# Bias terms in bf16, scatters on four banks and a new order ahead of the expert loop of a decoder layer

## The chip, the core and the metric

The kernel runs on one core of a Trainium2 chip. The metric is device time in microseconds (us) of one execution, as the median of several. The engines are TensorE (PE, whose weight loads are shown apart as PEld), VectorE (DVE), ScalarE (ACT), GpSimd (POOL) and SyncE (SP), which here only issues DMAs. Each takes its instructions in order; they meet at semaphores. ACT can issue DMAs too, on a queue of its own.

## What is computed

One decoder layer for 256 tokens of width 1024: attention with a relative-position bias, an output projection, a layer norm, then a mixture of 32 experts of which each token takes four, and a second layer norm. All inputs and weights are float32.

```
h = layer_norm(ALPHA * x + attention(x, w_in, w_out, rel_bias))
logits = h @ w_router + b_router
top_logit, top_e = top_k(logits, 4);  gate = softmax(top_logit)
for each expert e, for the rows xb of the tokens that chose it:
    g, u = split(xb @ w_gu[e] + b_gu[e])          # 1024 -> 2 x 1024
    g = min(g, 7);  u = clip(u, -7, 7)
    y = (g * sigmoid(1.702 * g) * (u + 1)) @ w_down[e] + b_down[e]
out = layer_norm(ALPHA * h + sum over the four experts of gate * y)
```

The weights of one expert are 8 MB (w_gu) and 4 MB (w_down), and all 32 experts are read, 403 MB in all.

## The kernel before

**Weights.** A pool of 13 slots of 2 MB holds the weights. Three of the slots are taken for the whole attention part (`xhl`, `BT_xT`, `QT_KTt`), the last two of them to the end, so 11 are left for the experts. `prefetch` issues one DMA on SP's queue for each slot that is given back by `done` or `drop`, in the order in which the pieces are used: for each expert four pieces of w_gu (`gu`) and two of w_down (`dn`), so 192 pieces of 2 MB. SP waits at each issue until the slot's last reader is through.

**Attention.** The projections run in two terms (a high part that ACT casts at line 176, a low part that DVE subtracts at line 165, in `split`), one half block ahead of PE. `rel_bias` writes the bias row to DRAM and reads it back spread over the partitions, both on SP's queue, ahead of further loads. The output projection runs in four chunks of `w_out` (`out_part(j, ...)`, j = 0 to 3); chunk j + 1 is split while chunk j is multiplied. Behind chunk 0 the expert biases are loaded: `b_gu` (32 x 2048) and `b_dn`, each once, into rows of the freed half `QT` (`biases`). 

**Router.** While the last chunk is multiplied, tokens come in two tiles t of 128 rows. `residual`, `count` and `Stats` make the norm; `rows_T` transposes the rows on PE and ACT copies them; `logits`, `top_experts` and `positions` give each token its place in its experts' blocks of 64. `stats[0].normal` runs on POOL for tile 0 and on ACT for tile 1. `first_gather(t)` then multiplies the rows by one-hot columns into banks tp0 and tp1 (opened by a matmul of zeros), so that the first pair's tokens lie transposed in `xg`. `filler(n)` issues n matmuls of zeros.

**Expert loop.** Experts go in pairs p, s = 0, 1. For expert e = 2p + s PE does: the bias (`stage1_bias`: four float32 matmuls of a one-hot over the 32 rows of `b_gu` into banks hg and hu), stage 1 (`stage1`, line 651: 64 columns of tokens against 512 columns of weights, two halves of the array side by side), then, while DVE and ACT make the SwiGLU, the scatter of the previous pair (`pair_scatter`, only s = 0: four matmuls into banks o0, o1, o0, o1, each added to `acc` by DVE at line 702) or the gather of the next pair (`pair_gather`, only s = 1: two quarters), then four transposes of the activation (`act_T`, line 668), a copy by ACT (line 669), and stage 2 (`stage2`, line 679). For s = 1 `pair_slots_T` transposes the pair's gates too. At e = 17 and 19 `add_residual` adds ALPHA * h and the down biases, at e = 21 `overflow_list` counts tokens beyond 64. Behind the loop, `more_blocks` would run such blocks, and the second norm ends the kernel.

**Order.** The schedule is manual: each engine runs its instructions in the order of the Python code.

Of the kernel before, what the change touches and what calls it, by code (L numbers as in the profile page):

```python
# [60 lines left out]
def tile_decoder_layer(ctx: ExitStack, tc, a, out):  # L61
# [152 lines left out]

    hctx = ExitStack()
# [14 lines left out]
    zeros = hp.tile([128, 512], BF, name="zeros")  # L230
# [27 lines left out]
    def rel_bias():  # L258
        pr = bank("tp2")
        nc.tensor.matmul(pr[:H, :256], rb, oh, start=True, stop=True)  # L260
        nc.vector.tensor_copy(rrow[:, 127:383], pr[:H, :256])
        nc.sync.dma_start(rd, rrow)
        nc.sync.dma_start(BT, bass.AP(tensor=rd.tensor, offset=rd.offset,
                                      ap=[[1, 128], [383, H], [1, S]]))
        nc.sync.dma_start(c, a["consts"])
        nc.sync.dma_start(router.rearrange("p k e -> p (k e)"), a["router"])

# [80 lines left out]
    def softmax(hh):  # L348
        ps = P[hh]
        p = hp.tile([128, 384], F32, name="p", bufs=3)  # L350
# [37 lines left out]
    for n in range(12):  # L388
# [69 lines left out]

    def router_weights():

        p = hp.tile([128, 384], F32, name="p", bufs=3)
        wb, cols = p[:, :256].rearrange("p (k e) -> p k e", k=KT), p[:, 256:320].rearrange("p (i e) -> p i e", i=2)
# [8 lines left out]
    for j in range(3):  # L471
        split_next(("out", 0, j))
        if j == 2:
            reserve[0] = 0
        for t in range(2):
            out_part(j, t, range(2 + t))
        done_split(("out", 0, j))
        if j == 1:
            router_weights()
        if j == 0:  # L480
            bgu, bdn, gT = biases[:NE], biases[NE:2 * NE, :D], biases[NE:2 * NE, D:D + S]
            nc.sync.dma_start(bgu, a["b_gu"])
            nc.sync.dma_start(bdn, a["b_dn"])
            bgu = bgu.rearrange("p (q c) -> p q c", q=4)
# [35 lines left out]
    def open_gather():  # L520

        for ps in first_ps:
            nc.tensor.matmul(ps, zeros[:, :128], zeros, start=True, stop=False)

    def filler(n):

        ps = bank("o0")
        for i in range(n):
            nc.tensor.matmul(ps, zeros[:, :128], zeros, start=i == 0, stop=i == n - 1)
# [19 lines left out]
    def stage1_bias(onehot_e):  # L549
        hgu = [bank(n) for n in ("hg", "hu")]  # L550
        for i in range(2):
            for s in range(2):
                nc.tensor.matmul(hgu[i][s * 64:(s + 1) * 64], onehot_e, bgu[:, 2 * i + s, :],  # L553
# [45 lines left out]
    pp = positions(0)  # L599
    hgu = stage1_bias(ident[:NE, 0:1].to_broadcast([NE, CAP]))  # L600
    top_experts(1)
    read_positions(0, pp)
    stats[1].normal_act(x[:, 1])
    pair_onehots(0, OH, slice(0, 1))
    first_ps = [bank("tp0"), bank("tp1")]
    open_gather()
    pp = positions(1)
    first_gather(0)
    read_positions(1, pp)
    pair_onehots(0, OH, slice(1, 2))  # L610
    filler(2)
# [17 lines left out]
    def pair_gather(OH):  # L629
        xg = mp.tile([128, KT, 2 * CAP], F32, name="xg")  # L630

        def quarter(q):
            ps = tp_tile()
# [31 lines left out]
    def act_T(act):  # L665
        ps = tp_tile()
# [18 lines left out]
    def pair_slots_T(Gd, GT=None):  # L685
        ps = tp_tile()
# [5 lines left out]
        if GT is None:  # L692
            GT = mp.tile([128, 2, 2, 2 * CAP], F32, name="GT")
# [9 lines left out]

    def pair_scatter(GT, Y, t, fresh):
        for cb in range(2):
            po = o_tile()
# [9 lines left out]
    def add_residual(i):  # L716

        cs = HALVES[i]
        if i == 0:
            ps = tp_tile()  # L720
            for t in range(2):
                nc.tensor.matmul(ps[NE:2 * NE, t * 128:(t + 1) * 128], gates[:, t], ident, start=True, stop=True)
            nc.scalar.copy(gT, ps[NE:2 * NE, :256])
# [36 lines left out]
    def more_blocks():  # L760
# [9 lines left out]
        with tc.For_i(0, n_reg, 1):  # L770
# [21 lines left out]
            sel_e = mp.tile([NE, 1], F32, name="sel_e")  # L792
            nc.vector.tensor_scalar(sel_e, c[:NE, C_PM:C_PM + 1], ec[:NE, 0:1], None, op0=OP.is_equal)
# [24 lines left out]
            hgu = stage1(lambda k: xg[:, k, :CAP], gu_chunk, stage1_bias(sel_e.to_broadcast([NE, CAP])),  # L818
# [16 lines left out]
    for p in range(NE // 2):  # L835
        ahead_pair = p + 1 < NE // 2
        for s in range(2):
            e = 2 * p + s
            look_ahead = ahead_pair and s == (p > 0)
            if e:  # L840
                hgu = stage1_bias(ident[:NE, e:e + 1].to_broadcast([NE, CAP]))
# [6 lines left out]
            if GT is not None and not s:  # L848
                for t in range(2):
                    pair_scatter(GT, Y, t, p == 1)  # L850
            if e in (17, 19):
                add_residual(e == 19)
            if e == 21:
                overflow_list()
            if look_ahead:
                xg_next, quarter = pair_gather(OH)
                quarter(0)
                if not s:
                    quarter(1)
            act_T(act)  # L860
            if s:
                GT = pair_slots_T(Gd)
                if ahead_pair:
                    if look_ahead:
                        quarter(1)
                    xg = xg_next
                    Gd = pair_gates(e + 1, OH)
# [101 lines left out]
```

## Time and profile before

| | us |
|---|---|
| median of 3 runs (lowest to highest) | 1072.66 (1072.33 to 1074.49) |
| the profiled execution, its own time | 1072.28 |
| its span, first to last instruction | 1070.5 |
| PE busy | 1016.2 (95%) |
| DVE, ACT, POOL busy | 264.1, 176.8, 7.4 |
| moved by DMA | 425.21 MB, 397 GB/s in the mean |

Steps are made against the span of 1070.5 us; 1.8 us lie around it. A busy share says what an engine did, not whether the end waited for it: PE is busy 95% of the span, and the DMA engines move 425 to 429 GB/s in nearly every slice of the expert loop. Which of the two sets the end is read from who waits for whom, and from when a weight lands against when it is used.

### The profile page before, as it was taken

Reading aid. Unit: us, or ns where it says so; the run is one execution under the profiler, and the core shown is the slowest. Engines: PE = TensorE matmul, PEld = TensorE weight load, DVE = VectorE, ACT = ScalarE, POOL = GpSimd, SP = SyncE. Lnnn points to the kernel's source line nnn. Section 1 sums busy time; section 2 is a strip of 40 time slices with the busy share of each in tenths; the row PEclk is TensorE's granted clock in tenths of the full one; section 3 lists DMA queues with packets and bytes.
Section 4 is the critical chain, followed back from the end, with each engine's and each line's share of the span. In section 5 each row is a group of like instructions: output and inputs, shape, how many; then the busy total and the mean of one; then the engine's idle time right before and its main releaser. Section 6 shows DMA issues by size and latency. Waiting matters only on the chain. (4 is left out here: it accounts for less than half of the span.)

```text
span 1070.5 us, 11658 instructions
## 1 busy us (share of the span) xinstructions
PE 1016.2 (95%) x5008; PEld 452.2 (42%) x5008; DVE 264.1 (25%) x554; ACT 176.8 (17%) x343; POOL 7.4 (1%) x8
## 2 busy tenths in 40 slices
PE   9999999999999999999999999999999999999994
PEld 8988743343434333343434343343434343434331
DVE  5576511212121211112121232212221212121204
ACT  5455311010101011010101010010101010101012
POOL 0000100000000000000000000000000000000001
PEclk9999899999999999999999999999999999999998
DMA  8995799999999999999999999999999999999931
GB/s 298 419 425 197 305 415 428 426 426 427 425 426 428 426 427 427 425 429 426 426 428 427 425 428 429 425 427 428 424 428 426 426 427 427 426 427 427 426 135 40
DMA packets 33108, 425.21 MB, mean 397 GB/s; under 512 B 3640, under 2 KB 5088, under 8 KB 7424
## 3 DMA queue, kind: packets, MB, share of 16 engines
q1 hardware_dynamic: 32784, 423.41, 93.9%
q10 hardware_dynamic: 272, 1.05, 0.3%
q8 instruction: 40, 0.66, 0.2%
q14 instruction: 12, 0.10, 0.0%
HBM read 423.38 MB, written 1.06 MB: 396 GB/s over the span
## 5 line engine op out<-in xcount | busy, mean ns | idle before, releaser
L651 PE MATMUL hg<-w,xg 128*64 128x512 f32 x960 | 248.2, 595 | 0.0
L651 PE MATMUL hu<-w,xg 128*64 128x512 f32 x960 | 246.6, 592 | 0.0
L679 PE MATMUL yp<-w,QT_KTt 128*64 128x512 f32 x1008 | 228.3, 599 | 10.6 <-ACT QT_KTt L669 10.6
L658 DVE TENSOR_SCALAR QT_KTt<-hg 128x512 f32<-128x512 f32 x32 | 22.1, 692 | 665.8 <-PE hg L651 665.8
L679 PEld LDWEIGHTS yp<-w,QT_KTt 128*64 128x64 f32 x1008 | 70.9, 138 | 145.5 <-issue 129.1
L651 PEld LDWEIGHTS hg<-w,xg 128*64 128x64 f32 x960 | 66.2, 137 | 144.4 <-issue 143.6
L651 PEld LDWEIGHTS hu<-w,xg 128*64 128x64 f32 x960 | 68.8, 137 | 137.2 <-issue 137.2
L659 ACT ACTIVATE QT_KTt<-QT_KTt 128x512 f32<-128x512 f32 x32 | 20.1, 629 | 459.8 <-DVE QT_KTt L658 459.8
L683 ACT COPY QT_KTt<-yp 64x512 f32<-64x512 f32 x63 | 36.5, 579 | 244.4 <-PE yp L679 237.4
L707 PE MATMUL o<-QT_KTt,GT 128*128 128x512 f32 x120 | 59.5, 618 | 12.8 <-DVE BT_xT L702 12.0
L637 PE MATMUL tp<-OH,BT_xT 128*128 128x128 f32 x480 | 62.5, 285 | 5.7 <-ACT xg L547 5.7
L637 PEld LDWEIGHTS tp<-OH,BT_xT 128*128 128x128 f32 x480 | 56.9, 195 | 20.3 <-issue 10.4
L165 DVE TENSOR_TENSOR whl<-w,whl 128x1024 fp32r<-128x1024 f32 (+1 forms) x36 | 38.3, 1103 | 22.6 <-ACT whl L176 22.6
L702 DVE TENSOR_TENSOR BT_xT<-o,BT_xT 128x512 f32<-128x512 f32 x60 | 40.0, 687 | 11.4 <-PE o L707 11.0
L707 PEld LDWEIGHTS o<-QT_KTt,GT 128*128 128x128 f32 x120 | 20.3, 188 | 51.8 <-DVE BT_xT L702 27.8
L176 ACT CAST whl<-w 128x1024 fp32r<-128x1024 f32 (+1 forms) x36 | 32.7, 955 | 14.3 <-PE tp L437 5.5
L553 PE MATMUL hg<-QT_KTt,c 32*64 32x512 f32 x128 | 35.0, 623 | 0.0
L545 DVE TENSOR_SCALAR xg<-tp,c 128x128 f32<-128x128 f32 x60 | 20.5, 405 | 53.7 <-PE tp L637 53.7
L553 PE MATMUL hu<-QT_KTt,c 32*64 32x512 f32 x128 | 33.6, 602 | 0.0
L669 ACT COPY QT_KTt<-tp 128x512 f32<-128x512 f32 x32 | 18.9, 590 | 73.6 <-PE tp L668 73.6
L547 ACT ACTIVATE xg<-tp,c 128x128 f32<-128x128 f32 x60 | 22.5, 456 | 34.0 <-PE tp L637 34.0
L668 PE MATMUL tp<-c,QT_KTt 128*128 128x128 f32 x128 | 20.3, 282 | 5.9 <-DVE QT_KTt L662 4.3
(250 smaller groups left out, 716.9 us busy)
## 6 DMA issues: line engine op xcount, KB each, us to landing
w<-in_w_gu SPq DMA_DIRECT2D x128, 2048.0 KB, 23.6
w<-in_w_dn SPq DMA_DIRECT2D x63, 2048.0 KB, 21.6
w<-in_w_in SPq DMA_DIRECT2D x3, 2048.0 KB, 15.8
w<-in_w_in SPq DMA_DIRECT2D x4, 1024.0 KB, 11.1
w<-in_w_out SPq DMA_DIRECT2D x2, 2048.0 KB, 24.8
w<-in_w_dn SPq DMA_DIRECT2D x4, 512.0 KB, 25.3
w<-in_w_in SPq DMA_DIRECT2D x4, 256.0 KB, 5.6
w<-in_w_in SPq DMA_DIRECT2D x2, 512.0 KB, 8.6
```

Source lines behind the costliest of these rows:

```text
L165: nc.vector.tensor_tensor(lo[:, s], w[:, s], hi[:, s].bitcast(F32), op=OP.subtract)
L176: nc.scalar.copy(o, i)
L545: nc.vector.tensor_scalar(o, i, g, b, op0=OP.mult, op1=OP.add)
L547: nc.scalar.activation(o, i, AF.Identity, scale=g, bias=b)
L553: nc.tensor.matmul(hgu[i][s * 64:(s + 1) * 64], onehot_e, bgu[:, 2 * i + s, :], start=True, stop=False)
L637: nc.tensor.matmul(ps[:, k * 128:(k + 1) * 128], h[:, t, kk * 128:(kk + 1) * 128], OH[:, t].rearrange("p s c -> p (s c)"), start=t == 0, s ...
L651: nc.tensor.matmul(hgu[i][s * 64:(s + 1) * 64], xg(k), w[:, kk, q * 512:(q + 1) * 512], start=False, stop=k == KT - 1)
L658: nc.vector.tensor_scalar(g7, hgu[0], LIMIT, None, op0=OP.min)
L679: nc.tensor.matmul(y_ps[s], aT[:, kk % 4, kk // 4, :], w[:, k, HALVES[s ^ swap]], start=kk == 0, stop=kk == KT - 1)
L683: copy(Y[s * 64:(s + 1) * 64, s ^ swap, :], y_ps[s])
L702: nc.vector.tensor_tensor(d, po, d, op=OP.add)
L707: nc.tensor.matmul(po, GT[:, cb, t, :], Y[:, cb, :], start=True, stop=True)
```

## The change

**Biases.** `b_gu` is loaded three times, into 96 rows. `bias_terms` makes three bf16 terms of it whose sum is the float32 value: ACT casts (96 x 2048), POOL subtracts (64 x 2048), ACT casts again (64 x 2048), POOL subtracts again (32 x 2048). The bias matmul then is one bf16 matmul over 96 rows, with a bf16 one-hot `sel`, in place of a float32 one over 32 rows. `bgu` lies in the memory of the softmax's three `p` tiles (pool `pp`, tag p3).

**Down bias.** `b_dn` is loaded later, at expert 15, into a weight slot `late` that is held until expert 19; `reserve` keeps that slot free from expert 14 on.

**Scatters and transposes.** The four scatters of a pair go to banks o0, o1, tp0, tp1, the fourth behind `act_T`. The gather's quarters have banks tp0 and tp1 for themselves, `act_T` tp2, `pair_slots_T` o0, and this comes ahead of `act_T`. The second quarter comes behind `act_T`. `xg` and `GT` move into `biases`.

**Attention and router.** The two DMAs of the relative bias go from SP's queue to ACT's, one and two half blocks later. The zeros shrink to 128 columns, read four times over. Fillers: two ahead of `positions(0)`, three behind `open_gather`, three instead of two ahead of `first_gather(1)`.

```
-        nc.sync.dma_start(rd, rrow)
-        nc.sync.dma_start(BT, bass.AP(tensor=rd.tensor, offset=rd.offset, ...))
+    def rel_bias_out():
+        nc.scalar.dma_start(rd, rrow)
+    def rel_bias_in():
+        nc.scalar.dma_start(BT, bass.AP(tensor=rd.tensor, offset=rd.offset, ...))
...
+        if n == 2:
+            rel_bias_out()
+        if n == 3:
+            rel_bias_in()
...
+    bgu = pp.tile([3 * NE, 2 * D], BF, name="bgu", tag="p3")
+    sel = small("sel", NE, 3 * NE, BF)
+    def bias_terms(i):
+        if i == 0:
+            nc.scalar.copy(bgu, biases[:3 * NE])
+            nc.gpsimd.tensor_tensor(biases[:2 * NE], biases[:2 * NE], bgu[:2 * NE], op=OP.subtract)
+            nc.vector.tensor_scalar(sel, e32[:3 * NE], c[:3 * NE, C_PM:C_PM + 1], None, op0=OP.is_equal)
+        else:
+            nc.scalar.copy(bgu[:2 * NE], biases[:2 * NE])
+            nc.gpsimd.tensor_tensor(bgu[NE:2 * NE], biases[NE:2 * NE], bgu[NE:2 * NE], op=OP.subtract)
...
         done_split(("out", 0, j))
+        if j == 0:
+            for i in range(3):
+                nc.sync.dma_start(biases[i * NE:(i + 1) * NE], a["b_gu"])
         if j == 1:
             router_weights()
-        if j == 0:
-            bgu, bdn, gT = biases[:NE], biases[NE:2 * NE, :D], biases[NE:2 * NE, D:D + S]
-            nc.sync.dma_start(bgu, a["b_gu"])
-            nc.sync.dma_start(bdn, a["b_dn"])
+            bias_terms(0)
+        if j == 2:
+            bias_terms(1)
...
+    first_ps = [bank("tp0"), bank("tp1")]
+    filler(2)
+    pp0 = positions(0)
+    hgu = stage1_bias(sel[:, 0:1].to_broadcast([3 * NE, CAP]))
...
     open_gather()
+    filler(3)
...
-    filler(2)
+    filler(3)
     first_gather(1)
...
-    def pair_scatter(GT, Y, t, fresh):
-        for cb in range(2):
-            po = o_tile()
+    def pair_scatter(GT, Y, t, fresh, cbs=range(2)):
+        for cb in cbs:
+            po = bank((("o0", "o1"), ("tp0", "tp1"))[t][cb])
...
-            if GT is not None and not s:
-                for t in range(2):
-                    pair_scatter(GT, Y, t, p == 1)
+            scatter = GT is not None and not s
+            if scatter:
+                pair_scatter(GT, Y, 0, p == 1)
+                pair_scatter(GT, Y, 1, p == 1, (0,))
+            reserve[0] = int(e == 14)
+            if e == 15:
+                late = slot("late")
+                nc.sync.dma_start(late[:NE, :D], a["b_dn"])
...
-            act_T(act)
             if s:
                 GT = pair_slots_T(Gd)
+            act_T(act)
+            if scatter:
+                pair_scatter(GT, Y, 1, p == 1, (1,))
+            if look_ahead:
+                quarter(1)
```

On ACT, from the cast of out-projection chunk 1 to the first copies of the transposed rows (`hg`, `hu`), there stood before (`whl` holds the split weights):

```order
L176 CAST whl<-w 128x1024 x2
L423 ACT_TABLE_LOAD
L176 CAST whl<-w 128x1024 x4
L176 COPY QT_KTt<-hg 128x4x128
L176 COPY QT_KTt<-hu 128x4x128
```

And now stands on ACT at the same place:

```order
L176 CAST whl<-w 128x1024 x2
L433 ACT_TABLE_LOAD
L176 CAST whl<-w 128x1024 x2
L475 CAST bgu<-QT_KTt 96x2048
L176 CAST whl<-w 128x1024 x2
L479 CAST bgu<-QT_KTt 64x2048
L176 COPY QT_KTt<-hg 128x4x128
L176 COPY QT_KTt<-hu 128x4x128
```

The first cast of the biases has moved in ahead of the casts of chunk 3, and the second ahead of the copies of the transposed rows. On POOL the two subtractions stand ahead of the normalisation of tile 0 (line 207).

On PE, from the end of stage 1 of expert 2 to the bias of expert 3, there stood before (`o` and `tp` are banks, `yp` stage 2's):

```order
L651 MATMUL hu<-w,xg 64x512 x2
L707 MATMUL o_1522<-QT_KTt,GT 128x512
L707 MATMUL o_1525<-QT_KTt,GT 128x512
L707 MATMUL o_1528<-QT_KTt,GT 128x512
L707 MATMUL o_1531<-QT_KTt,GT 128x512
L668 MATMUL tp_1534<-c,QT_KTt 128x128 x4
L679 MATMUL yp<-w,QT_KTt 64x512 x16
L553 MATMUL hg<-QT_KTt,c 64x512 x2
```

And now stands on PE at that place:

```order
L677 MATMUL hu<-w,QT_KTt 64x512 x2
L733 MATMUL o_1531<-QT_KTt 128x512
L733 MATMUL o_1534<-QT_KTt 128x512
L733 MATMUL tp_1537<-QT_KTt 128x512
L694 MATMUL tp_1540<-c,QT_KTt 128x128 x4
L733 MATMUL tp_1546<-QT_KTt 128x512
L705 MATMUL yp<-w,QT_KTt 64x512 x16
L577 LDWEIGHTS sel
L577 MATMUL hg<-bgu,sel 64x512
```

The fourth scatter has moved behind the transposes, the last two have other banks, and the bias reads `bgu`.

## Rows read from the trace of the kernel before

**Rows 1.** Page, section 2: GB/s moved by the DMA engines, 40 equal slices.
```profile
GB/s 298 419 425 197 305 415 428 426 426 427 425 426 428 426 427 427 425 429 426 426 428 427 425 428 429 425 427 428 424 428 426 426 427 427 426 427 427 426 135 40
```

**Rows 2.** Waits of PE: engine, line, waited for: total us, times, longest us.
```profile
PE o L707 <- DVE BT_xT L702: 12.0, 14, 1.2
```

**Rows 3.** Windows: stretch us, length, busy us by engine (instructions), PE clock, DMA share, GB/s.
```profile
101.00:102.00 1.00, 0.94 (x7) 0.72 (x6) 0.41 (x3) 0.59 (x1) 0.00 (x0) 1.00 1.02 213
118.00:127.00 9.00, 8.66 (x36) 5.32 (x36) 3.13 (x19) 1.52 (x2) 0.70 (x1) 0.62 0.97 407
173.00:178.00 5.00, 4.76 (x20) 1.97 (x22) 0.90 (x4) 1.07 (x2) 0.00 (x0) 0.66 1.02 433
972.00:999.00 27.00, 26.50 (x140) 11.33 (x138) 4.85 (x12) 4.25 (x9) 0.00 (x0) 1.00 1.01 427
```

**Rows 4.** Timeline of SP's queue, three issues: start us, us, engine, line, operation, tile.
```profile
94.46 0.38 SPq L482 DMA_DIRECT2D QT_KTt<-in_b_gu  x1
132.80 0.33 SPq L138 DMA_DIRECT2D w<-in_w_dn  x1
991.73 0.33 SPq L138 DMA_DIRECT2D w<-in_w_gu  x1
```

**Rows 5.** DMA view of those issues, same order: KB, last number us to landing.
```profile
QT_KTt<-in_b_gu SPq DMA_DIRECT2D x1, 256.0 KB, 9.3
w<-in_w_dn SPq DMA_DIRECT2D x1, 2048.0 KB, 8.9
w<-in_w_gu SPq DMA_DIRECT2D x1, 2048.0 KB, 27.6
```

**Rows 6.** Timeline of PE: experts 2 and 3, last expert: start us, us, line, form.
```profile
182.73 1.07 PE L553 MATMUL hg<-QT_KTt,c 32*64 32x512 f32 x4
184.59 1.08 PE L651 MATMUL hg<-w,xg 128*64 128x512 f32 x4
198.48 1.98 PE L707 MATMUL o<-QT_KTt,GT 128*128 128x512 f32 x4
201.27 1.98 PE L707 MATMUL o<-QT_KTt,GT 128*128 128x512 f32 x4 [0.81 <-DVE BT_xT L700]
204.36 1.08 PE L679 MATMUL yp<-w,QT_KTt 128*64 128x512 f32 x4 [0.67 <-ACT QT_KTt L669]
227.13 2.05 PE L637 MATMUL tp<-OH,BT_xT 128*128 128x128 f32 x16
232.75 0.65 PE L679 MATMUL yp<-w,QT_KTt 128*64 128x512 f32 x2
239.77 1.07 PE L553 MATMUL hg<-QT_KTt,c 32*64 32x512 f32 x4
1039.11 1.03 PE L651 MATMUL hg<-w,xg 128*64 128x512 f32 x4
```

**Rows 7.** Timeline ahead of the expert loop: ACT, PE and POOL.
```profile
101.41 2.00 ACT L176 CAST whl<-w 128x1024 fp32r<-128x1024 f32 x2 [3.56 <-PE tp L437]
107.30 0.40 PE L434 MATMUL o<-whl,xhl 128*128 128x512 f32 x1
112.05 0.58 ACT L176 COPY QT_KTt<-hg 128x512 f32<-128x512 f32 x1 [8.64 <-PE hg L454]
114.57 4.13 POOL L207 TENSOR_SCALAR BT_xT<-BT_xT,rs_a 128x512 f32<-128x512 f32 x2 [114.12 <-DVE rs_a L203]
126.80 0.59 PE L529 MATMUL o<-zeros 128*128 128x512 bf16 x2
127.23 1.95 PE L535 MATMUL tp<-BT_xT 128*128 128x128 f32 x16
129.11 1.08 PE L651 MATMUL hg<-w,BT_xT 128*64 128x512 f32 x4
```

**Rows 8.** Line 898 by source: POOL multiplication, min/median/max ns.
```profile
L898 POOL TENSOR_TENSOR BT_xT<-BT_xT,gb_sq x2: 1402/1550/1698, 1060.3 to 1062.3; 128x512 f32<-128x512 f32 x2
```

**Rows 9.** Page, section 5, one group: busy us, mean ns, idle before.
```profile
L165 DVE TENSOR_TENSOR whl<-w,whl 128x1024 fp32r<-128x1024 f32 (+1 forms) x36 | 38.3, 1103 | 22.6 <-ACT whl L176 22.6
```

More of the change, by code (lines that the diff above doesn't have):

```diff
@@ L229, in tile_decoder_layer @@
     rrow = hp.tile([H, 383], F32, name="rrow")
-    zeros = hp.tile([128, 512], BF, name="zeros")
+    zeros = hp.tile([128, 128], BF, name="zeros")
+    zeros4 = zeros[:, None, :].to_broadcast([128, 4, 128])
+    p3 = pp.tile([128, 3, 384], F32, name="p3", tag="p3")
     router = hp.tile([128, KT + 1, NE], F32, name="router")
@@ L349, in softmax @@
         ps = P[hh]
-        p = hp.tile([128, 384], F32, name="p", bufs=3)
+        p = p3[:, hh % 3]
         st = hp.tile([128, 8], F32, name="sst", bufs=3)
@@ L457, in tile_decoder_layer @@
     sums = small("sums", 2 * NE)
+    bgu = pp.tile([3 * NE, 2 * D], BF, name="bgu", tag="p3")
[8 more added lines that the diff above has]
+            nc.gpsimd.tensor_tensor(bgu[NE:2 * NE], biases[NE:2 * NE], bgu[NE:2 * NE], op=OP.subtract)
     def router_weights():
-        p = hp.tile([128, 384], F32, name="p", bufs=3)
-        wb, cols = p[:, :256].rearrange("p (k e) -> p k e", k=KT), p[:, 256:320].rearrange("p (i e) -> p i e", i=2)
+        wb, cols = first[:, 1536:1792].rearrange("p (k e) -> p k e", k=KT), first[:, 1792:1856]
+        cols = cols.rearrange("p (i e) -> p i e", i=2)
         ps = bank("yp")
@@ L522, in open_gather @@
         for ps in first_ps:
-            nc.tensor.matmul(ps, zeros[:, :128], zeros, start=True, stop=False)
+            nc.tensor.matmul(ps, zeros, zeros4, start=True, stop=False)
     def filler(n):
@@ L528, in filler @@
         for i in range(n):
-            nc.tensor.matmul(ps, zeros[:, :128], zeros, start=i == 0, stop=i == n - 1)
+            nc.tensor.matmul(ps, zeros, zeros4, start=i == 0, stop=i == n - 1)
     def first_gather(t):
@@ L629, in pair_gather @@
     def pair_gather(OH):
-        xg = mp.tile([128, KT, 2 * CAP], F32, name="xg")
+        xg = biases[:, :1024].rearrange("p (k c) -> p k c", k=KT)
         def quarter(q):
-            ps = tp_tile()
+            ps = bank(("tp0", "tp1")[q])
             for k in range(4):
@@ L665, in act_T @@
     def act_T(act):
-        ps = tp_tile()
+        ps = bank("tp2")
         for j in range(4):
@@ L685, in pair_slots_T @@
     def pair_slots_T(Gd, GT=None):
-        ps = tp_tile()
+        ps = bank("o0")
         for cb in range(2):
@@ L692, in pair_slots_T @@
         if GT is None:
-            GT = mp.tile([128, 2, 2, 2 * CAP], F32, name="GT")
+            GT = biases[:, 1024:1536].rearrange("p (b t c) -> p b t c", b=2, t=2)
         nc.scalar.copy(GT, ps.rearrange("p (b t c) -> p b t c", b=2, t=2))
@@ L718, in add_residual @@
         cs = HALVES[i]
+        bdn, gT = late[:NE, :D], late[:NE, D:D + S]
         if i == 0:
@@ L721, in add_residual @@
             for t in range(2):
-                nc.tensor.matmul(ps[NE:2 * NE, t * 128:(t + 1) * 128], gates[:, t], ident, start=True, stop=True)
-            nc.scalar.copy(gT, ps[NE:2 * NE, :256])
+                nc.tensor.matmul(ps[:NE, t * 128:(t + 1) * 128], gates[:, t], ident, start=True, stop=True)
+            nc.scalar.copy(gT, ps[:NE, :256])
         ps = tp_tile()
@@ L857, in tile_decoder_layer @@
                 quarter(0)
-                if not s:
-                    quarter(1)
-            act_T(act)
             if s:
                 GT = pair_slots_T(Gd)
[L863 to L867, printed above, removed]
+            act_T(act)
[3 more added lines that the diff above has]
+                quarter(1)
+            if s and ahead_pair:
+                xg = xg_next
+                Gd = pair_gates(e + 1, OH)
             if e == NE - 2:
```

26 lines of the change are left out of this document (12 added, 14 removed).

## The prediction

> **What bounds the kernel now.** I read the page's line of GB/s first [rows 1]. From the seventh slice on the DMA engines move 424 to 429 GB/s, until they are done near 1026 us; a window late in the loop shows their share at 1.01 [rows 3]. So the stream of weights never pauses in the expert loop. Then I read what PE waits for. Its longest wait is for DVE to empty a scatter bank [rows 2], and no wait in the loop is for a weight. So PE is never short of weights either: two things run beside each other at nearly one pace, and PE ends last.
>
> The pace of the stream: the twelfth piece is issued at 132.80, when PE has freed its first slot 3.7 us into stage 1 (which begins at 129.11 [rows 7]), and lands 8.9 us later, at 141.7. The last gate-up piece, number 190, is issued at 991.73 and lands 27.6 us later, at 1019.3 [rows 4, 5]. That is 178 pieces in 877.6 us, 4.93 us each, 29.6 us per expert of six. The pace of PE: experts 2 and 3 take from 182.73 to 239.77, 57.04 us, 28.5 us each [rows 6]. PE starts behind by eleven landed pieces and gains 1.1 us per expert, but at the end it still is late: it begins the piece that landed at 1019.3 only at 1039.11 [rows 6]. These 19.8 us are all that a faster PE can win, since it cannot begin a piece that has not landed. From 1039.11 to the end of the span there are 31.4 us, in the same code before and after.
>
> **The change, part by part.** *The loop on PE.* The float32 bias takes 182.73 to 184.59, 1.86 us [rows 6]. For four bf16 matmuls of 512 columns the nearest row is the filler: two start 0.43 us apart from what follows, so 0.21 each [rows 7], 0.86 in all if halves of the array do not overlap and 0.43 if they do. I take 0.86: 1.0 saved per expert. Even experts: from the first scatter to stage 2 it is 5.88 us (198.48 to 204.36), with waits of 0.81 for a bank and 0.67 for ACT's copy [rows 6]. With four banks, three scatters of 0.9, the transposes (0.5) and the fourth scatter, beside which ACT copies, make 4.1; so 1.75 saved. Odd experts: 5.62 us (227.13 to 232.75); the second quarter of the gather (1.9) now covers ACT's copy, about 0.75 saved. A pair saves 2.0 + 1.75 + 0.75 = 4.5 us and takes 52.5, 26.3 per expert, well under the stream's 29.6. Over 16 pairs that would be 72 us, but only 19.8 can be had: PE catches up where 129.1 + 4.38 n = 141.7 + 4.93 (n - 11), at piece 76, in expert 13, and waits for weights from there, some 3.3 us per expert.
>
> *The stream.* `b_gu` twice more falls where slots are full, ahead of the loop. `b_dn` moves into the stream: 128 KB at the 213 GB/s that the loads into 32 rows reached [rows 3] are 0.6 us. The slot held from expert 14 to 19 costs nothing: at 27.6 us from issue to landing over five pieces are in flight [rows 5], and with a faster PE more; if that cover were gone, a piece would come 4.9 us late. Banks for the quarters, `xg`, `GT` and the later down bias bring no new wait that I can see.
>
> *Ahead of the loop.* What matters here is when stage 1 begins, since the first free slot starts the stream again. ACT and POOL take their work in order, and the bias terms stand in that order. (1) `b_gu` was issued at 94.46 and landed at 103.8 [rows 4, 5]. 384 KB were loaded there, now 768; at 213 GB/s that is 1.8 us more, 105.6. (2) ACT casts 96 x 2048 then: as long as two casts of 1024, 2.0 [rows 7], to 107.6. Only behind it come the casts of chunk 3, which ran at 101.41 and which PE wants at 107.30 [rows 7]. DVE's low parts follow at 1.1 each [rows 9]; PE's first six matmuls on the chunk end near 111.4 in place of 108.7, and all that follows moves by 2.7. (3) POOL subtracts from 107.7, for P. ACT's second cast (2.0) waits for that, and behind it the copies of the transposed rows, ready at 112.05 + 2.7 = 114.75; this costs little. POOL's second subtraction ends at 109.8 + 2P, and the normalisation of tile 0 queued behind it (4.13 [rows 7]) at 113.9 + 2P. Then half a gather (1.0), three fillers (0.6) and the second gather (1.9 [rows 7]): stage 1 at 117.5 + 2P. (4) PE's own chain: 129.11 + 2.7, less what the cheaper bias and the fillers can give back. [...]
>
> P is not in the trace. The same operation on 512 columns took 1.40 and 1.70 us [rows 8]; four times that is 5.6 to 6.8, and four halves of line 207 (4.13 for two) are 8.3. So stage 1 begins at 128.7, 131.1 or 134.1; below P = 5.4 the chain (4) decides. I take 5.9, between the two values of the same operation: 129.3. A part of the gathers will run at the lower clock as before, 0.8: 130.1, so d = 1.0 later than before, between -0.7 and 5.0.
>
> [...]
>
> *Relative bias on ACT's queue*: two issues more on ACT. PE had no wait for it and has the same distance to the first softmax; nothing. If the read back came later than the first softmax it would delay that head, but two half blocks lie between.
>
> *Sum.* Last gate-up piece 1019.3 + d 1.0 + `b_dn` 0.6 = 1020.9; + 31.4 = 1052.3 of span; + 1.8 around it = 1054.1. The profiled execution (1072.28) lies 0.4 below the median, within its spread. I say 1054.
>
> **Rivals.** *POOL slow within the rows.* P = 8.3 gives d = 5.0 and 1058; with both gathers at the lower clock (2 us) 1060. For it: DVE is at work beside POOL, one operand is bf16. Against: the rows of the same operation.
>
> *The clock.* PE will wait in each of the last experts. At 173 to 178 us, behind a pause of 2 us, the clock's mean was 0.66 [rows 3], which cost 1.7 us. If this came once or twice per expert, PE's 26.3 would become 28 to 29.7, still about the stream's pace, and a PE that falls behind waits no more; what shows is a late last expert, 1057 to 1060. Against: only in few of such pauses did the clock fall. [...]
>
> [...]
>
> *Full gain of PE.* 1072.3 - 72 + d: 1001. It needs a stream above 429 GB/s, which no slice shows.
>
> *Slower.* The subtractions stand ahead of the start of the stream, and the time is 1042.3 + 2P with the lower clock's 0.8. From P = 16.1 on, 7.8 ns per column against 2.7 to 4.1 in the rows, it is over 1074.4; at P = 18 it is 1078. For it: 64 rows with one bf16 operand, a form that the trace does not have.
>
> *It does not do what it says.* If bf16 were no cheaper for the bias, the pair would still save 2.5 us, 40 in all, above 19.8. Only if the bank waits stayed too is there no change.
>
> **How the numbers follow.** Forecast 0.62 (1051 to 1057), POOL slow 0.13, the clock 0.09, no blocking 0.08, full gain 0.02, slower 0.04, no change 0.02. The range runs from 1050 to 1061. Faster by over 0.2%, about what a measurement of this kernel can tell from no change, 0.94; within that 0.02; slower 0.04.
>
> **What would show it.** In the profile after: PE waits for DMAs of `w` in the second half, 50 us or more in all, and its busy share falls; GB/s as before to the end; stage 1 of expert 0 near 130 and of the last piece 1 us behind its landing. ACT's cast of `bgu` waits for its DMA near 105 and chunk 3's casts come behind it. Stage 1 much later would put P too low; a stream with pauses in the loop would make the reasoning wrong, and so would a last piece begun well after it landed.

## The result and the profile after

| | before | after |
|---|---|---|
| median (lowest to highest), us | 1073.58 (1072.33 to 1074.70), 4 runs | 1087.15 (1086.92 to 1090.02), 4 runs |
| after / before, 95% interval | | 1.0133 (1.0111 to 1.0155) |
| profiled execution: span, us | 1070.5 | 1085.3 |
| stage 1 of expert 0 begins | 129.11 | 158.89 |
| the last gate-up piece is begun | 1039.11 | 1048.68 |
| from there to the end of the span | 31.4 | 36.6 |

The change makes the kernel 1.3% slower; the forecast was 1.7% faster. The loop did what was forecast, but began 28.8 us later than forecast, and 5.2 us more were lost behind it. The page's line of GB/s of the kernel after, 40 equal slices, against [rows 1]:

```profile
GB/s 358 422 243 152 161 297 406 428 427 428 428 426 428 428 425 430 427 427 429 426 429 428 413 423 426 428 428 427 427 428 427 428 429 428 428 428 426 429 372 40
```

The slices of the loop read as before; the low stretch ahead of it (slices 3 to 6) is longer. Waits of PE in the kernel after, the four longest (engine, line, waited for: total us, times, longest us), against [rows 2]:

```profile
PE hg L677 <- DMA w<-in_w_gu: 54.2, 48, 2.3
PE o L310 <- DVE QT_KTt L320: 24.5, 1, 24.5
PE o L916 <- issue: 5.0, 1, 5.0
PE o L445 <- DVE whl L165: 3.8, 1, 3.8
```

The first line is what was forecast: PE is short of weights, in 48 places, and the waits for scatter banks are gone. That the stream sets the end is read from the last gate-up piece: its issue, its landing 39.1 us later, near 1048.6, and PE's start on it at 1048.68:

```profile
1009.55 0.33 SPq L138 DMA_DIRECT2D w<-in_w_gu  x1
...
w<-in_w_gu SPq DMA_DIRECT2D x1, 2048.0 KB, 39.1
...
1048.68 1.08 PE L677 MATMUL hg<-w,QT_KTt 128*64 128x512 f32 x4
```

The other three lines are three losses that the forecast had not. **The first, in the attention:** who makes DVE late there is read from the timeline (start us, us, engine, line, operation, tile [idle before it <- released by]):

```profile
30.00 0.39 ACTq L272 DMA_DIRECT2D BT_xT<-rd  x1
...
67.24 0.62 DVE L359 SCALAR_TENSOR_TENSOR p<-hg,BT_xT 128x128 f32<-128x128 f32 x2 [28.47 <-DMA BT_xT<-rd]
...
68.86 0.55 PE L310 MATMUL o<-xhl,whl 128*128 128x256 f32 x1 [24.49 <-DVE QT_KTt L320]
```

DVE's first softmax waits for the read back of the relative bias, and PE for a copy that stands behind that softmax in DVE's order. The DMA view gives KB and us from issue to landing, for the kernel after and then for the kernel before:

```profile
BT_xT<-rd ACTq DMA_DIRECT2D x1, 1024.0 KB, 37.1
QT_KTt<-in_b_gu SPq DMA_DIRECT2D x3, 256.0 KB, 9.8
```

```profile
BT_xT<-rd SPq DMA_DIRECT2D x1, 1024.0 KB, 5.8
```

The same megabyte takes 37.1 us on ACT's queue and 5.8 on SP's. On SP's queue it was issued at 23.40, ahead of the further loads, and all 1179 packets that moved from 23.4 to 29.2 us were smaller than 2 KB: no weights ran beside it. On ACT's queue it was issued at 30.00, and SP's queue was full of weights by then. The later issue alone would have cost nothing: DVE was ready for the read back at 38.77 (67.24 less its wait of 28.47), and 5.8 us from 30.00 is 35.8. What happens beside the weights is seen in the packets of a window of the kernel after, 40 to 50 us (queue: packets, MB, share of the 16 engines' time; q1 is SP's, q10 ACT's):

```profile
q1 hardware_dynamic: 271, 3.95, 93.3%
q10 hardware_dynamic: 271, 0.28, 8.0%
```

In this window the two queues go one packet for one packet. SP's packets are rows of the weights of up to 16 KB (14.6 KB in the mean), those of the read back 1 KB; so the read back gets one byte for fourteen of SP's: 27.1 packets per us, 1024 of them in 37.8 us if it goes on so. That this comes so near to 37.1 is partly luck, since only 61 packets of ACT's queue pass in the first 6 us, and the last 200 pass nearly alone, behind 64 us. **The second loss, ahead of the loop:** timeline of ACT, POOL and DVE in the kernel after, against [rows 7]:

```profile
131.27 1.90 ACT L475 CAST bgu<-QT_KTt 96x2048 bf16<-96x2048 f32 x1 [7.55 <-DMA QT_KTt<-in_b_gu]
133.07 1.99 ACT L176 CAST whl<-w 128x1024 fp32r<-128x1024 f32 x2
133.25 4.06 POOL L476 TENSOR_TENSOR QT_KTt<-QT_KTt,bgu 64x2048 f32<-64x2048 f32 x1 [132.79 <-ACT bgu L475]
134.15 5.38 DVE L165 TENSOR_TENSOR whl<-w,whl 128x1024 fp32r<-128x1024 f32 x2 [5.97 <-ACT whl L176]
137.33 1.90 ACT L479 CAST bgu<-QT_KTt 64x2048 bf16<-64x2048 f32 x1 [2.27 <-POOL QT_KTt L476]
139.31 4.17 POOL L480 TENSOR_TENSOR bgu<-QT_KTt,bgu 32x2048 bf16<-32x2048 f32 x1 [2.01 <-ACT bgu L479]
```

DVE's two low parts of chunk 3 take 5.38 us, where such a pair takes 2.4 elsewhere (5.4 less 2.4 is 3.0). One by one, the first takes 4.24 and the second 1.21. They stand beside POOL's first subtraction, which ends at 137.31; two times 1.18 from there is 139.67, and they end at 139.53. So it looks as if DVE stood still, within the first, until POOL was through. **The third loss, behind the loop:** PE's next matmul behind the last stage 2, and the branch of PE over `more_blocks` (on PE's own list of control instructions, PEldq; durations min/median/max in ns, first and last start), in the kernel after, and the branch in the kernel before:

```profile
1067.94 5.70 PE L916 MATMUL o<-QT_KTt 128*128 128x512 f32 x8 [5.00 <-issue]
...
L797 PEldq COMPARE_BRANCH  x3: 97/196/3549, 1059.2 to 1067.7; - x3
```

```profile
L770 PEldq COMPARE_BRANCH  x3: 101/187/325, 1049.5 to 1054.8; - x3
```

One branch of PE takes 3.55 us where none took over 0.33 before. The eight scatters behind it then run for 5.70 us, in place of 3.90 before, at a lower granted clock (0.69 in the mean from 1063 to 1074 us; in the kernel before 1.00 from 1053 to 1060).

### The profile page after: what moved, and what is told of

The parts are those of the page before. It is cut to its first block, busy times and chain, and to the rows that moved or that the text cites. A ratio compares the mean times of both kernels' runs of the same rounds, so it can differ in the third digit from the quotient of the medians.

```text
span 1085.3 us, 11473 instructions
## 1 busy us (share of the span) xinstructions
PE 975.1 (90%) x4886; PEld 450.4 (41%) x4886; DVE 265.6 (24%) x555; ACT 180.5 (17%) x345; POOL 15.7 (1%) x10
## 5 line engine op out<-in xcount | busy, mean ns | idle before, releaser
L677 PE MATMUL hg<-w,QT_KTt 128*64 128x512 f32 x960 | 250.8, 599 | 54.5 <-DMA w<-in_w_gu 54.2
L677 PE MATMUL hu<-w,QT_KTt 128*64 128x512 f32 x960 | 248.6, 594 | 0.0
L677 PEld LDWEIGHTS hg<-w,QT_KTt 128*64 128x64 f32 x960 | 66.0, 137 | 194.9 <-issue 127.0
L677 PEld LDWEIGHTS hu<-w,QT_KTt 128*64 128x64 f32 x960 | 71.2, 137 | 135.7 <-issue 135.7
L165 DVE TENSOR_TENSOR whl<-w,whl 128x1024 fp32r<-128x1024 f32 (+1 forms) x36 | 41.2, 1187 | 29.4 <-ACT whl L176 29.4
L310 PE MATMUL o<-xhl,whl 128*128 128x256 f32 x48 | 15.0, 312 | 25.1 <-DVE QT_KTt L320 24.5
L569 DVE TENSOR_SCALAR QT_KTt<-tp,c 128x128 f32<-128x128 f32 x60 | 20.5, 405 | 44.1 <-PE tp L663 44.1
L733 PE MATMUL tp<-QT_KTt 128*128 128x512 f32 x60 | 30.7, 593 | 0.0
L733 PE MATMUL o<-QT_KTt 128*128 128x512 f32 x60 | 29.8, 618 | 0.0
L571 ACT ACTIVATE QT_KTt<-tp,c 128x128 f32<-128x128 f32 x60 | 22.6, 457 | 36.3 <-PE tp L663 36.3
L686 DVE TENSOR_SCALAR hu<-hu 128x512 f32<-128x512 f32 x32 | 22.4, 700 | 3.1 <-PE hu L677 0.2
L688 DVE SCALAR_TENSOR_TENSOR QT_KTt<-hu,QT_KTt 128x512 f32<-128x512 f32 x32 | 22.1, 691 | 1.1
## 6 DMA issues: line engine op xcount, KB each, us to landing
w<-in_w_gu SPq DMA_DIRECT2D x128, 2048.0 KB, 39.1
w<-in_w_dn SPq DMA_DIRECT2D x63, 2048.0 KB, 39.1
```

Of the source, the lines that this page charges most:

```text
L165: nc.vector.tensor_tensor(lo[:, s], w[:, s], hi[:, s].bitcast(F32), op=OP.subtract)
L569: nc.vector.tensor_scalar(o, i, g, b, op0=OP.mult, op1=OP.add)
L571: nc.scalar.activation(o, i, AF.Identity, scale=g, bias=b)
L677: nc.tensor.matmul(hgu[i][s * 64:(s + 1) * 64], xg(k), w[:, kk, q * 512:(q + 1) * 512], start=False, stop=k == KT - 1)
L686: nc.vector.tensor_scalar(u7, u7, LIMIT, -LIMIT, op0=OP.min, op1=OP.max)
L688: nc.vector.scalar_tensor_tensor(sg, u7, 1.0, g7, op0=OP.add, op1=OP.mult)
```

## The experiments

Times are medians; the kernel before is 1072 to 1073 us in each group. A kernel with one run has only its one time.

**1. The changed kernel with the relative bias on SP's queue.**

```
+        nc.sync.dma_start(rd, rrow)
+        nc.sync.dma_start(BT, bass.AP(tensor=rd.tensor, offset=rd.offset, ...))
         nc.sync.dma_start(c, a["consts"])
...
-        if n == 2:
-            rel_bias_out()
-        if n == 3:
-            rel_bias_in()
```

> The changed kernel with one part undone: the two DMAs of the relative bias go back to SP's queue, at the place that they had before. Theory A (the read back of the bias row on ACT's queue landed 37 us after its issue, and PE stood still for 24.5 us behind it): PE's 24.5 us wait behind DVE's line 320 is gone, the read back lands some 6 us after its issue, stage 1 of expert 0 begins near 133 us in place of 158.9, and the time falls by about 26 us, to 1060 to 1062: faster than before. Rival B (the loss comes from the bias terms ahead of the loop, or from the slots): stage 1 still begins later than 150 us and the time stays above 1073.

Measured: 1060.8 us (1060.11 to 1061.73, 4 runs), ratio to before 0.9881 (0.9861 to 0.9900). The read back lands after 5.6 us, stage 1 begins at 133.63, PE's wait of 24.5 us is gone. So 26 us of the changed kernel's time are the move of one DMA, and everything else together is a gain of 12. The two smaller losses stay: waits of 3.8 us for L165 and of 4.9 in the tail.

**2. The kernel before with only this move.** The same two DMAs on ACT's queue, nothing else.

> The kernel before with that one part alone: the two DMAs of the relative bias on ACT's queue, everything else as it was. Theory A: the read back lands 35 to 40 us after its issue, PE waits 22 to 26 us at about 45 us, all later work moves by as much: 1096 to 1100 us. Rival B: within 3 us of the kernel before.

Measured: 1100.62 us, one run, 28 us over before and 0.6 over what was expected. Waits of PE, longest first, then the DMA:

```profile
PE o L307 <- DVE QT_KTt L317: 24.4, 1, 24.4
```

```profile
BT_xT<-rd ACTq DMA_DIRECT2D x1, 1024.0 KB, 37.3
```

The move alone makes the loss, with or without the rest of the change. Both experiments move queue and place together; ACT's queue at the old, earlier place was not run.

**3. The read back in two parts, on ACT's queue.**

```
-        nc.scalar.dma_start(BT, bass.AP(tensor=rd.tensor, offset=rd.offset, ap=[[1, 128], [383, H], [1, S]]))
+        for h0 in (0, 4):
+            nc.scalar.dma_start(BT[:, h0:h0 + 4], bass.AP(..., offset=rd.offset + h0 * 383, ap=[[1, 128], [383, 4], [1, S]]))
```

> The changed kernel, with the read back on ACT's queue cut into two DMAs of four heads each; the first softmax needs the first of them alone. Theory A1 (the DMA engines take the two queues in turn, one packet of ACT's rows of 1 KB for one of SP's rows of 16 KB): the first half, with half of the rows, lands after half of the time, 18 to 20 us after its issue, the second after about 37; PE's wait falls from 24.5 to 5 to 8 us, the time to 1067 to 1071. Rival A2 (ACT's transfer gets nothing until SP's queue has run empty near 64 us): both halves land near 65 us, PE waits 24 us as before, 1085 to 1089.

Measured: 1074.71 us, one run, between the two. PE's wait is 11.6 us in place of 24.5: the first half lands 24.5 us after its issue, with SP's queue still full, so the read back does not wait for an empty queue. The size was missed. 512 packets at 27 per us are 19 us; but in the first 6 us (30 to 36) only 63 packets of the read back pass, against 161 in the next 6, and that start had been left out.

**4. The weight loads around the read back in rows of half the size**, so that a packet of the read back waits for less.

```
-            fetch(1 if len(todo) > 1 else 4)
+            fetch(4 if len(todo) == 1 else 2 if len(todo) > 188 else 1)
```

> The changed kernel, with the weight DMAs that SP issues ahead of and during the read back cut in two, so that their rows are 8 KB in place of 16 KB. Theory A1 (in turn, packet for packet): each turn of ACT's queue costs half, the read back lands 19 to 23 us after its issue in place of 37, PE waits 7 to 12 us in place of 24.5, the time is 1068 to 1075. Rival A2 (the transfer waits for SP's queue to run empty): the bytes queued are the same, the landing stays at 34 to 38 us and the time at 1085 to 1089.

Measured: 1088.87 us, one run. The time is that of the rival and not of the theory, but it settles neither: the write of the bias row was issued ten us later than in the changed kernel, and the read back only at 42.34. It landed 25.0 us after that, between the two forecasts (19 to 23, 34 to 38), when SP's queue ran dry. Its packets tell more. The window of 46 to 56 us:

```profile
q1 hardware_dynamic: 490, 3.60, 87.3%
q10 hardware_dynamic: 490, 0.50, 14.7%
```

Again one for one, now 49 per us in place of 27, beside packets of SP's of 7.3 KB in the mean in place of 14.6: in these two windows the size of the other queue's packet sets the pace.

**5. The first experiment's kernel with the bias terms later.** ACT's first cast and POOL's first subtraction behind chunk 3's casts, POOL's second subtraction behind the normalisation of tile 0, the bias of expert 0 behind the last gather.

> The changed kernel with the relative bias back on SP's queue (as in the first experiment) and the bias terms later: ACT's first cast and POOL's first subtraction behind the casts of out-projection chunk 3, ACT's second cast just ahead of tile 0's normalisation, POOL's second subtraction behind it, the bias matmul of expert 0 behind the last gather. Theory: in the first experiment PE waited 0.85 + 3.8 us ahead of stage 1 because the cast stands ahead of chunk 3's casts (2.0) and DVE's two low parts of chunk 3 took 2.7 us each beside POOL's subtraction, where they take 1.18 otherwise. Then the pair takes 2.4 us again, PE's wait of 3.8 us is gone, stage 1 begins at 126 to 128 in place of 133.6, and as the stream of weights sets the end all of this arrives there: 1053 to 1055 us. Rival: the low parts are slow for another reason (the loads into 32 rows beside them, or their place in DVE's order); then they still take 5.4 and the time stays at 1058 to 1061.

Measured: 1060.04 us (1059.03 to 1060.50, 6 runs): the rival's time, but not by its reason. The pair of low parts takes 2.4 us again and PE is 8 us ahead by the first logits. Then this comes (timeline of DVE and POOL):

```profile
117.70 0.25 DVE L523 SCALAR_TENSOR_TENSOR lg<-lg,rs_a,sums 128x32 f32<-128x32 f32 x1
...
118.91 4.05 POOL L481 TENSOR_TENSOR bgu<-QT_KTt,bgu 32x2048 bf16<-32x2048 f32 x1
...
119.66 3.35 DVE L523 SCALAR_TENSOR_TENSOR lg<-lg,rs_a,sums 128x32 f32<-128x32 f32 x1
```

The same operation on 32 columns takes 0.25 us for tile 0 and 3.35 for tile 1, ending at 123.01, when POOL's subtraction has ended (122.96). PE waits 3.7 us for its result, and the gather behind that is slow (3.76 us for 16 matmuls, 1.95 for the next 16; in the ninth kernel such a gather takes 3.75, where the granted clock is 0.52 in the mean from 120 to 127 us). The wait has moved. Both stretched rows, this one and the low part of the second loss (4.24 us for 1.2), have two operands in SBUF; this one ends 0.05 us behind a subtraction on POOL, the other 1.08, near its own 1.2. Beside POOL's normalisation (114.69 to 118.83, one operand in SBUF) the row at 117.70 took its usual 0.25.

**6. The fifth without the loop for further blocks.** That part of the computation is left out.

> The fifth experiment's kernel without the loop for tokens beyond an expert's first 64 (left out: that part of the computation; here the loop is passed with no turn). Theory: the 4.9 us that PE stands still between its last stage 2 and the last scatters are the fetch of its instructions behind the loop that is jumped over (two packets of 16 KB on the instruction queue fall into this gap, one in the kernel before, whose gap was 1.7). Then the gap is under 1.5 us, the last eight scatters keep the full clock (3.9 us in place of 5.7), and the time is 4 to 6 us below the fifth experiment's. Rival: the gap belongs to the end of the stream or to the wait for the copies of stage 2's result, and stays at 4 to 5 us, the time within 1 us of the fifth's.

Measured: 1054.73 us, one run, 5.3 under the fifth. PE behind the last stage 2:

```profile
1037.21 3.90 PE L917 MATMUL o<-QT_KTt 128*128 128x512 f32 x8 [0.82 <-DVE QT_KTt L711]
```

The gap and the slow scatters belong to the jump over this loop.

**7. The fifth with the old scatters and order**: of the loop's changes the bf16 bias is left, with the later down bias and the separate banks of the gathers and the transposes.

> The fifth experiment's kernel with the scatters on two banks and all four ahead of the transposes, and the gathers and transposes in the old order: of the changes in the loop only the bias in bf16 is left. Theory (the prediction's): the stream of weights bounds the loop at 59.2 us per pair, and PE with the bf16 bias alone needs 57.0 - 2 x 1.43 = 54.2. So the time is within 2 us of the fifth experiment's, and PE's waits for weights shrink from 53 us to 10 to 25. Rival: the order and banks carry the gain, PE sets the end again: above 1065 us, with no waits for weights.

Measured: 1061.33 us, one run, 1.3 over the fifth. PE's first waits:

```profile
PE hg L679 <- DMA w<-in_w_gu: 29.0, 26, 1.7
PE o L735 <- DVE BT_xT L730: 11.2, 14, 0.8
```

A pair takes PE 53.3 us here before it runs into the stream (235.34 to 288.67); 29 us of slack are left.

**8. The kernel before with the other half**: new scatters and order, bias in float32, nothing changed ahead of the loop.

> The kernel before with the other half alone: scatters on banks o0, o1, tp0, tp1, the fourth behind the transposes, the gather's second quarter behind them too, bank tp2 for the transposes; the bias stays in float32, and nothing ahead of the loop changes. Theory: PE needs 57.0 - 2.5 = 54.5 us per pair, less than the stream's 59.2, so this half too wins all there is: stage 1 at 129.1, the last gate-up piece landed at 1019.3, and 31.4 to 36.6 us behind it, 1052.5 to 1057.7 us, with 5 to 25 us of waits for weights. Rival: the order alone saves nothing, for the bank waits only move: 1070 to 1074 us.

Measured: 1058.08 us, one run. A pair takes 54.2 us (181.19 to 235.43), and PE waits for weights:

```profile
PE hg L651 <- DMA w<-in_w_gu: 18.0, 18, 1.3
PE o L883 <- issue: 5.0, 1, 5.0
```

So either half of the loop's changes brings PE under the stream's pace, and both together bring no more time, as far as one run each can tell. The time is 0.4 over the expected range, with the tail's gap in it.

**9. The first experiment's kernel with nothing of the bias terms ahead of the loop.** Expert 0 takes its bias in float32; the terms are made by ACT and DVE during its stage 1.

```
-            bias_terms(0)
-        if j == 2:
-            bias_terms(1)
...
-            nc.gpsimd.tensor_tensor(biases[:2 * NE], biases[:2 * NE], bgu[:2 * NE], op=OP.subtract)
+            nc.vector.tensor_tensor(biases[:2 * NE], biases[:2 * NE], bgu[:2 * NE], op=OP.subtract)
...
     Gd = pair_gates(0, OH)
     GT = None
+    bias_terms(0)
+    bias_terms(1)
```

> The changed kernel with the relative bias on SP's queue, and nothing of the bias terms ahead of the loop: expert 0 takes its bias in float32 from the third copy of b_gu, and the casts (ACT) and subtractions (DVE in place of POOL) run beside stage 1 of expert 0. Theory: in the first and fifth experiments what held PE was DVE, whose instruction with two operands in SBUF stood still until POOL's subtraction was through (5.4 in place of 2.4 us for the pair of low parts, 3.35 in place of 0.25 for a logits step of 32 columns, both ending within 0.1 us of what POOL's end gives). Without a subtraction on POOL neither row is stretched, PE has no wait over 1 us there, stage 1 begins at 126 to 128.5 (131.6 in the fifth), and the time is 1055 to 1057.5 us. Rival: something else of the changed part ahead of the loop holds it (the larger load, the fillers), and stage 1 stays at 131 to 134, the time at 1059 to 1061.

Measured: 1058.14 us (1054.88 to 1058.83, 5 runs), 0.6 over the range. With no subtraction on POOL no row of DVE is stretched and PE has no such wait, but stage 1 begins at 129.60 in the profiled execution. What is left is the clock: window of 118 to 126 us (length, busy us by engine, granted clock, DMA share, GB/s), here and then in the tenth kernel, whose code up to there is the same:

```profile
118.00:126.00 8.00, 8.00 (x33) 4.92 (x32) 2.83 (x17) 1.52 (x2) 0.36 (x1) 0.64 1.01 423
```

```profile
118.00:126.00 8.00, 8.00 (x55) 5.60 (x54) 2.75 (x16) 2.06 (x4) 0.25 (x1) 1.00 1.00 421
```

With the full clock stage 1 begins at 126.24, 3.4 us earlier, within what was expected. Both happen in the same code.

**10 to 12. The ninth with 32, 64 or 96 matmuls of one column more** in expert 12, where they move PE's later instructions by 64, 128 or 192 places.

> The ninth experiment's kernel with 32 matmuls of one column more on PE in expert 12 (64 instructions with their weight loads; a result that nobody reads). PE waits for weights behind that place, so they cost nothing by themselves. Theory: PE's branch over the loop for further blocks takes 3.5 us here and 0.3 in the kernel before because of where its target lies in the instruction memory, so a shift of the program can take the 3.5 us away: gap of 1.7 us ahead of the last eight scatters, which then take 3.9, and 4 to 6 us less than the ninth experiment. Rival: the place does not matter, the gap stays at 4.7 to 5.0 us, the time within 1 us of the ninth's. Of the three shifts (this and the next two) the theory needs at least one to show the short branch.

> As the tenth, with 64 matmuls of one column (128 instructions). Theory: one of the three shifts shows the short branch, 4 to 6 us less than the ninth experiment. Rival: gap of 4.7 to 5.0 us in all three, the time within 1 us of the ninth's.

> As the tenth, with 96 matmuls of one column (192 instructions). Theory: one of the three shifts shows the short branch, 4 to 6 us less than the ninth experiment. Rival: gap of 4.7 to 5.0 us in all three, the time within 1 us of the ninth's.

Measured: 1051.24 (1049.64 to 1055.17), 1051.06 (1049.86 to 1054.04) and 1051.76 us (1050.41 to 1053.61), 4 runs each; ratios to before 0.9815 (0.9789 to 0.9842), 0.9804 (0.9780 to 0.9829) and 0.9813 (0.9792 to 0.9835). All three show the short branch; the tenth:

```profile
1032.01 3.90 PE L917 MATMUL o<-QT_KTt 128*128 128x512 f32 x8 [1.84 <-DVEq L792]
...
L792 PEldq COMPARE_BRANCH  x3: 97/187/414, 1026.5 to 1031.8; - x3
```

They are 6.4 to 7.1 us under the ninth, more than the 4 to 6 expected. Against the ninth's profile (gap 5.2, scatters 5.38) the tail gives 4.9 us; the other 3.4 of the 8.3 us between the two spans are the clock just told of. So the shift itself is worth 4.9 us by the traces, and the medians may differ by more because they mix executions with either clock: the ninth's five runs spread over 4 us, the tenth's four over 5.5.

**13 and 14. The ninth with 128 and with 8 such matmuls**, 256 and 16 places. An estimate from the page of the kernel before: its instruction queue q8 moved 40 packets, 0.66 MB, so 16 KB each, and its PE has 10016 instructions (5008 matmuls and as many weight loads); if that queue is PE's, about 250 go to a packet, and 256 places are about one packet.

> [...] Theory (the place of the branch's target within a packet decides): a shift by a whole packet brings the long branch back, 3.5 us or more, and a gap of 4.7 to 5.3 us ahead of the last eight scatters. Rival (the added instructions themselves, or the time they take, make the fetch come in time): the branch takes 0.3 to 0.5 us and the gap is 1.8, as in the tenth to twelfth.

> As the ninth, with 8 matmuls of one column more (16 instructions). Theory (place within a packet): three shifts of 64, 128 and 192 instructions were all short, so the long stretch is narrow, under 64 instructions of 256; 16 can fall on either side, so the branch alone tells less than in the run before. Rival (number of added instructions): still long, 3.5 us. A short branch here would speak against the rival.

Measured: 1060.77 and 1059.45 us, one run each; gaps of 5.2 and 5.0 us. The branch of the thirteenth:

```profile
L792 PEldq COMPARE_BRANCH  x3: 97/192/3781, 1032.6 to 1041.4; - x3
```

Shifts of 0, 16 and 256 are long, of 64, 128 and 192 short: a shift of 256 brings the long branch back, so it is not the number of added instructions, and the place is what fits all six. What place each branch has is not in the trace, so why the eighth kernel's is long, with as many matmuls as the kernel before (but 42 more instructions on all engines together, 11700 against 11658), stays open. That the long branch waits for a fetch of instructions was not shown; in the gap two packets of 16 KB pass on the instruction queue in the kernel after (1062.94 to 1067.94 us) and one in the kernel before (1053.31 to 1055.01).

One thing in these six traces is not explained. From 118 to 126 us, long ahead of the branch, the granted clock is 1.00 in the tenth kernel, with the short branch, and the two gathers of the eleventh and of the twelfth take 2.03 and 1.95 us there, where the ninth's first takes 3.75; it is 0.64, 0.60 and 0.57 in the three with the long branch. With one trace of each this may be chance: the kernel before (0.58) and the fifteenth (0.63) have the low clock there and a short branch.

**15. The eighth with 32 such matmuls.**

> The eighth experiment's kernel (the kernel before with the new scatters and order alone, bias in float32) with 32 matmuls of one column more on PE in expert 12. Theory: the branch becomes short, and the time is 4 to 6 us under the eighth's 1058.1, 1051 to 1054, for the stream bounds the loop with the float32 bias too. Rival: without the bias terms PE is too near the stream's pace (waits for weights of 18 us in the eighth), and the padding, which costs PE 2 to 4 us once, brings the time to 1055 or more.

Measured: 1051.77 us (1049.64 to 1052.59, 4 runs), ratio 0.9807 (0.9786 to 0.9828); branch 0.39 us, gap 1.8, waits for weights 14.8 us. The new scatters and a shift, without the bias terms, are as fast as all of the change without its losses.

## Why the prediction was wrong

**The step that failed** is "Relative bias on ACT's queue: nothing". It looked at PE's distance to the first softmax and took for granted that the DMA itself would last as long on the other queue; its duration there was in no row, and no bounds were given for it. It went from 5.8 to 37.1 us. In its place the runs showed a DMA that shares the engines packet for packet with a full queue of weights (271 to 271 in 10 us). Experiments 1 and 2 price that at 26 and 28 us, from both sides, and of the 28.8 us by which stage 1 came later than forecast it makes 25.3 (158.89 against 133.63 in the first experiment). The condition was named ("if the read back came later than the first softmax") but cost as one head's delay; in truth PE stood behind it for 24.5 us, since DVE's copies for PE stand behind the softmax in its order.

**Ahead of the loop**, without that, stage 1 began at 133.63 in place of 130.1. The terms were right one by one and wrong together. `b_gu` landed when forecast (ACT's cast at 105.93 against 105.6), the cast took 1.90 (2.0 taken), the subtractions 4.06 and 4.16 us: P had been taken as 5.9, and lies below its lowest bound of 5.6. By the prediction's own sum PE's chain (4) decides then, with stage 1 between 128.4 (its d of -0.7) and 131.8 (129.11 + 2.7), and not at 133.63. The 128.4 is 131.8 less 3.4, an estimate (9.00 us at a mean clock of 0.62 [rows 3] are 3.4 more than the same work takes at 1.00); the P of 5.4 rests on it, and the range's lower end of 1050 takes 3.4 from 129.1 (stage 1 at 125.7). No run shows that the cheaper bias and the fillers give these 3.4 back; what the runs showed is stage 1 at 129.60 with a clock of 0.64 and at 126.24 with 1.00 (experiments 9 and 10), with nothing of the bias terms ahead. But the shift of chunk 3 was put at 2.7 us, from ACT's order alone; DVE stood still beside POOL for another 3.0, and PE, which waited, went on at the lower clock (0.54 in the mean from 136 to 143 us in the kernel after). That a busy POOL could hold DVE was in no step. The trace of before has a row of it: on one column line 905 took 0.97 us at 1060.73, beside line 898 on POOL, and 0.22 at 1065.42. Experiments 5 and 9 show the cause: moved to another place the subtraction held another instruction, and gone from POOL it held none.

**The loop** went as forecast. Timeline of PE in the kernel after, an even and an odd expert, against [rows 6]:

```profile
223.29 1.98 PE L733 MATMUL o<-QT_KTt 128*128 128x512 f32 x4
...
227.37 7.09 PE L705 MATMUL yp<-w,QT_KTt 128*64 128x512 f32 x32
234.28 0.39 PE L577 MATMUL hg<-bgu,sel 96*64 96x512 bf16 x2
234.50 0.38 PE L577 MATMUL hu<-bgu,sel 96*64 96x512 bf16 x2
...
248.55 2.05 PE L663 MATMUL tp<-OH,BT_xT 128*128 128x128 f32 x16
...
253.19 7.09 PE L705 MATMUL yp<-w,QT_KTt 128*64 128x512 f32 x32
260.11 0.39 PE L577 MATMUL hg<-bgu,sel 96*64 96x512 bf16 x2
```

From scatter to stage 2 it is 4.08 us (4.1 forecast), on the odd side 4.64 (4.87), and the bias takes 0.43, the lower of its two bounds; the odd expert takes 25.83 (26.3). The waits for weights came to 54.2 us ("50 us or more"). That the stream sets the end and pays only 19.8 us of all that PE saves is shown by experiments 7 and 8: a half of the saving gives the same time. The first freed slot was used at 162.59, 29.8 us later than before, and the last piece was begun 886.1 us after that; before, it landed after 886.5.

**The tail** was carried over as 31.4 us, "the same code before and after". It took 36.6: the gap ahead of the last scatters was 3.3 us longer, by the branch, and the scatters took 1.8 more at the lower clock. The code was the same, its place in the program not (experiments 10 to 14).

**The rivals.** The time lies beyond all of them. "Slower" had the right direction, a late start of the stream, and a wrong cause (P was small). "The clock" had a chance of 0.09 for its waits in the loop; from 300 to 600 us the granted clock was 1.00 in the mean, with such waits in it, the longest of 2.3 us. With the bias on SP's queue the time of 1060.8 lies at the upper end of the range, and with the other two losses taken away too at 1051. That this is 3 us from the forecast's 1054 is in part luck: it takes the full clock ahead of the loop, with which stage 1 began at 126.24 in the tenth and not at 130.1.

## What to carry to other kernels

A DMA moved to a second queue is a new DMA: price it by packets against packets, for here one with rows of 1 KB got 0.28 MB beside the 3.95 MB of a full queue with rows of up to 16 KB. Before work goes to POOL, ask which instructions of DVE with two operands in SBUF fall beside it (here 4.24 us in place of 1.2, and 3.35 in place of 0.25), and follow PE to its end. And when one engine is freed under a stream that bounds, do no more than reaches the stream: here a new order of the scatters gave all that there was (0.981), and the bias terms added nothing that could be measured (medians of 1051.1 to 1051.8 with them and 1051.8 without, where the runs of one kernel spread over 3 to 5.5 us).

## What the runs showed of the hardware

- ACT's queue of DMA, with rows of 1 KB, moved as many packets as SP's full queue beside it: 271 and 271 in 10 us with rows of up to 16 KB (the kernel after), 490 and 490 with rows of 8 KB (experiment 4). 1 MB of such rows took 37.1 us beside the weights (37.3 in experiment 2) and 5.6 to 5.8 ahead of them.
- Beside a tensor_tensor on POOL, instructions of DVE with two operands in SBUF were stretched: 4.24 us for 1.2 (the kernel after), 3.35 for 0.25 (experiment 5). Beside POOL's tensor_scalar such a one took its usual 0.25 (experiment 5).
- PE's branch over a loop that turns zero times took 0.33 us in the kernel before and 0.33 to 0.42 in experiments 10 to 12 and 15, and 3.52 to 3.78 in the kernel after and in experiments 1, 5, 8, 9, 13 and 14. Shifts of the ninth kernel by 64, 128 and 192 places took the long one away, one by 256 brought it back. The eight scatters took 3.90 us behind a short one and 5.34 to 5.77 behind a long one; in the kernel after the granted clock was 0.70 in the mean in the gap (1063 to 1068 us) and 0.68 from there to 1074.
- The clock ahead of the loop was 0.64 in one profiled execution and 1.00 in another, from 118 to 126 us, in kernels with the same code up to there (experiments 9 and 10): 3.4 us. What decides it is open.
